# Gates and branch merges of two transformer blocks, token-major in place of feature-major

## The chip, the cores and the metric

The kernel runs on one core of one Trainium2 chip. The metric is the device time of one execution in microseconds (us), taken as the median of several runs; lower is better.

## What is computed

256 tokens with 1024 features go through two blocks, all in float32. Each block projects the normalised input, computes two branches, gates each branch with a sigmoid, merges them by up-projections, and projects the sum out. Cut to this:

```python
# block 1
xn = rms_norm(x, norm1_w)
z = xn @ w_in            # q, k, v ..., xr, gr, g_a (1024 columns), g_b (1024 columns)
attn = nsa_attention(...)                      # 512 features
rnn = rg_lru_branch(...)                       # 1024 features
merged = sigmoid(g_a) * (attn @ w_up_attn) + sigmoid(g_b) * (rnn @ w_up_rnn)
x = x + merged @ w_out
x = x + square(relu(rms_norm(x, norm2_w) @ mlp_w1)) @ mlp_w2
x = rms_norm(x, final_norm_w)
# block 2: a gated feed-forward, then
u = rms_norm(h, mix_norm); z = u @ w_in_2      # qa ka va qb kb vb, ga, gb
merged = sigmoid(ga) * (ya @ w_branch_a) + sigmoid(gb) * (yb @ w_branch_b)   # 512 features each
h = h + merged @ w_out_2
# a second gated feed-forward and a last norm
```

## The kernel before

**Precision.** Every float32 matmul is made of three fp32r products: weights and inputs are each split into a rounded part ("hi") and the rest ("lo"), and hi x hi, hi x lo and lo x hi are summed in PSUM.

**Weights.** All weights lie in one DRAM stream `ws` in the order in which the program uses them. The sync queue (SP) loads chunks of two pieces of 1024 columns into three `raw` buffers (`load_to`, L226). `split_to` (L238) splits each piece: ScalarE (ACT) writes `whi` (L248), VectorE (DVE) writes `wlo` (L249), five buffers each. `wt` (L253) asks for the split of the piece two ahead of the one that is wanted.

**Matmul forms.** `mmx` (L296) keeps a 128x128 weight tile stationary and streams 256 token columns, three matmuls for each (128 input rows, 128 output features); the result is feature-major (features on partitions). `mm3` (L290) is the opposite: 128 tokens of the input are stationary and weight columns are streamed; the result is token-major. `mm_wide` (L302) streams hi and lo of the input together (512 columns), then 256 more.

**Gates.** `fm1` (L1010, block 1) and its like `z2` (block 2) run `ga` and `gb` through `mmx`, one bank for each pair p of feature tiles (p = 0 to 3). The evacuation is a DVE multiplication by the per-token reciprocal norm `rbA`, broadcast along partitions, and an ACT tanh (`ev_tanh`, L984 and L985; `ev_g2`, L1408 and L1409). sigmoid(z) is 0.5 (1 + tanh(z/2)); the 0.5 is applied after the output projection.

**Merges.** `merge` (L1033) builds `m1` and `m2`. For each pair p, `mm` runs branch a or b through `mmx`, then DVE computes (1 + tanh) * branch in place (L1044). When both branches of p are done, `fin` adds them (L1050) and `split2` (L325) splits the sum into hi (ACT, L329) and lo (DVE, L330): that is `m`, feature-major, which `out_proj` (L1087, tags `wo`, `wo_0_*`) streams through `fm` (L336). `fm` with lead=2, hold=2 starts the first two pairs with the first 6 of 8 input tiles k before it finishes either.

**Order.** ORDER_1 and ORDER_2 (L156, L159) list the steps of each block by name: `ga1` is pair 1 of gate a, `mb2` pair 2 of branch b's merge, `at3` the next three pieces of attention. A scheduler then fixes one static order for each engine. PSUM has eight banks: `g` 3, `s` 2, `t` 2, `o` 1; matmuls of gates and merges use `g`, transposes use `t`.

Of the kernel before, what the change touches and what calls it, by code (L numbers as in the profile page):

```python
# [374 lines left out]
def build(nc, tc, d, out, es, dbg=None):  # L375
# [236 lines left out]
    def vg():  # L612
# [6 lines left out]
        hc = G.small((P, 2), "halfcol")  # L619
        nc.vector.tensor_scalar(out=hc, in0=S["colA"], scalar1=0.5, scalar2=None, op0=ALU.mult)  # L620
# [358 lines left out]
    def ev_tanh(key):  # L979
        def ev(p, b):  # L980
            if p == 0:
                S[key] = G.big(key)
            t = pair(S[key], p)
# [49 lines left out]
    def merge(tag, wa, wb, ka, kb, xa, xb, rows_a, rows_b):  # L1033

        done = []

        def mm(p, sfx, nk, x, key):
            b = G.ps("g", f"{tag}{sfx}{p}")
            for k in range(nk):
                for nn in range(2):  # L1040
                    wh, wl = G.wt((tag + sfx, k, 2 * p + nn))
                    G.mmx(b[:, nn * T:(nn + 1) * T], wh, wl, x(k), k == 0 and nn == 0, k == nk - 1)
            t = pair(S[key], p)
            nc.vector.scalar_tensor_tensor(out=t, in0=t, scalar=1.0, in1=v2(b), op0=ALU.add, op1=ALU.mult)  # L1044

        def fin(p):
            if tag not in S:
                S[tag] = Parts(G.big, tag)
            t = pair(S["tga"], p)
            nc.vector.tensor_tensor(out=t, in0=t, in1=pair(S["tgb"], p), op=ALU.add)  # L1050
            G.split2(*S[tag].pair(p), t)

        def branch(p, sfx):
            w, nk, x, rows = ((wa, ka, xa, rows_a), (wb, kb, xb, rows_b))[sfx == "b"]
            G.step(lambda: mm(p, sfx, nk, x, "tg" + sfx),
                   [((tag + sfx, k, n), w, rows(k), [(n * P, P)]) for k in range(nk) for n in (2 * p, 2 * p + 1)])
            if p in done:
                G.step(lambda: fin(p))
            done.append(p)
# [343 lines left out]
    def ev_g2(key):  # L1403
        def ev(p, b):
            if p == 0:
                S[key] = G.big(key + "2")
            t = pair(S[key], p)
            nc.vector.scalar_tensor_tensor(out=t, in0=v2(b), scalar=0.5, in1=two(S["rbA"]), op0=ALU.mult, op1=ALU.mult)  # L1408
            nc.scalar.activation(out=t, in_=t, func=AF.Tanh)  # L1409
        return ev  # L1410

# [8 lines left out]
    def take2():  # L1420
# [6 lines left out]
    g2a, g2b = ev_g2("tga"), ev_g2("tgb")  # L1427
    m2 = merge("m2", "w_branch_a_2", "w_branch_b_2", 4, 4, lambda k: S["ya"].both(k), lambda k: S["yb"].both(k), plain, paired)
# [4 lines left out]
        "ga": lambda p: z2("ga2", 2304, p, g2a), "gb": lambda p: z2("gb2", 3328, p, g2b),  # L1433
        "ma": lambda p: m2(p, "a"), "mb": lambda p: m2(p, "b"), "at": lambda n: [take2() for _ in range(n)]}
# [147 lines left out]
```

## Time and profile before

| | |
|---|---|
| device time, three runs | 966.12, 966.34, 968.51 us (median 966.34) |
| the profiled execution | 966.17 us, of which its span is 964.4 us |
| mean granted TensorE clock | 0.996 |
| TensorE (PE) busy | 948.3 us, 98% of the span |
| DVE busy | 728.4 us, 76% |
| ACT busy | 585.0 us, 61% |

The profile page gives busy time by engine, the span in 40 slices, the chain of work that ended last, and the costliest groups of instructions. A view of waits lists, by engine and line, idle time and what ended it; a timeline lists single instructions; a table of windows gives busy time and the granted TensorE clock of chosen stretches. Matmuls are pipelined, so a record's own duration overlaps its neighbours'; the price of one in a stream is the length of an unbroken piece of the chain divided by its count.

### The profile page before, as it was taken

How to read it: one execution, taken by the hardware profiler on the slowest of the kernel's cores; microseconds unless marked ns; L12 is line 12 of the kernel's file. 1: busy time of each engine (PE TensorE's matmuls, PEld its weight loads, DVE VectorE, ACT ScalarE, POOL GpSimd, SP SyncE). 2: the span in 40 equal slices, each digit the busy share in tenths (PEclk: the TensorE clock that was granted, in tenths of full speed). 3: DMA queues.
4: the chain of work that ended last, by engine and by line, in shares of the span. 5: the costliest groups of instructions: out<-in, count | busy, mean ns of one | idle time of the engine just before them, and what ended most of it. 6: DMA issues, size and time to landing. Idle time of an engine off the chain costs nothing.

```text
span 964.4 us, 15990 instructions
## 1 busy us (share of the span) xinstructions
PE 948.3 (98%) x6310; PEld 870.1 (90%) x6310; DVE 728.4 (76%) x1219; ACT 585.0 (61%) x961; POOL 42.0 (4%) x71
## 2 busy tenths in 40 slices
PE   8999999999999999999999999899999999999997
PEld 7989999998888888888888889899999888888897
DVE  7898879879888655679888657779767878777553
ACT  6795898546767544566555445678764565555441
POOL 6100000000000000030000200000000000000000
PEclk9999999999999999999999999999999999999999
DMA  9575442634545555565555755353334565555541
GB/s 331 188 268 212 138 154 104 245 131 178 215 175 193 201 177 196 195 207 180 203 187 182 240 180 177 136 204 108 113 132 172 178 201 204 185 175 183 186 141 45
DMA packets 26556, 174.03 MB, mean 180 GB/s; under 512 B 3313, under 2 KB 3569, under 8 KB 7281
## 3 DMA queue, kind: packets, MB, share of 16 engines
q1 hardware_dynamic: 24912, 169.80, 49.8%
q0 software_dynamic: 1136, 2.63, 1.4%
q8 instruction: 49, 0.80, 0.3%
q10 hardware_dynamic: 432, 0.58, 0.2%
q14 instruction: 27, 0.21, 0.1%
HBM read 171.43 MB, written 1.05 MB: 179 GB/s over the span
## 4 chain that ended last, share of the span: by engine, by line
PE 93%; ACT 4%; DVE 1%; issue 1%; DMA 0%; POOL 0%; POOLq 0%; ACTq 0%
PE f L306 17%; PE w L306 12%; PE f L307 9%; PE w L307 6%; PE ld L294 6%; PE ga L300 5%; PE fd L306 4%; PE gb L300 4%; PE wo L306 3%; PE m1b L300 2%; PE fd L307 2%; PE xr L300 2%; PE gr L300 2%; PE wo L307 2%; PE va L294 1%; PE ka L300 1%
## 5 line engine op out<-in xcount | busy, mean ns | idle before, releaser
L249 DVE TENSOR_TENSOR wlo<-raw,whi 128x1024 fp32r<-128x1024 f32 (+3 forms) x322 | 389.1, 1210 | 168.0 <-ACT whi L248 150.3
L248 ACT ACTIVATE whi<-raw 128x1024 fp32r<-128x1024 f32 (+3 forms) x322 | 335.7, 1047 | 285.6 <-PE w L306 64.2
L306 PE MATMUL f<-u,whi 128*128 128x512 f32 x704 | 246.7, 396 | 0.0
L307 PE MATMUL f<-u,wlo 128*128 128x256 f32 x704 | 196.5, 279 | 0.0
L306 PEld LDWEIGHTS f<-u,whi 128*128 128x128 f32 x704 | 132.0, 188 | 31.3
L307 PEld LDWEIGHTS f<-u,wlo 128*128 128x128 f32 x704 | 132.7, 188 | 0.1
L306 PE MATMUL w<-u,whi 128*128 128x512 f32 x256 | 88.8, 392 | 0.0
L306 PE MATMUL w<-hid,whi 128*128 128x512 f32 x256 | 88.8, 391 | 0.0
L307 PE MATMUL w<-hid,wlo 128*128 128x256 f32 x256 | 71.7, 280 | 0.0
L307 PE MATMUL w<-u,wlo 128*128 128x256 f32 x256 | 71.3, 280 | 0.0
L306 PE MATMUL fd<-f1h,whi 128*128 128x512 f32 x176 | 61.1, 394 | 0.0
L294 PE MATMUL ld<-whi,f2h 128*128 128x256 f32 (+1 forms) x264 | 59.0, 319 | 0.0
L306 PEld LDWEIGHTS w<-hid,whi 128*128 128x128 f32 x256 | 47.9, 187 | 10.5
L306 PEld LDWEIGHTS w<-u,whi 128*128 128x128 f32 x256 | 47.7, 187 | 10.3
L300 PE MATMUL ga<-u,whi 128*128 128x256 f32 x256 | 48.2, 284 | 1.1 <-ACT whi L248 1.1
L307 PE MATMUL fd<-f1h,wlo 128*128 128x256 f32 x176 | 48.8, 277 | 0.0
L307 PEld LDWEIGHTS w<-u,wlo 128*128 128x128 f32 x256 | 48.3, 189 | 0.2
L307 PEld LDWEIGHTS w<-hid,wlo 128*128 128x128 f32 x256 | 48.4, 189 | 0.0
L300 PE MATMUL gb<-u,whi 128*128 128x256 f32 x256 | 48.2, 284 | 0.0
L294 PEld LDWEIGHTS ld<-whi,f2h 128*128 128x128 f32 x264 | 44.0, 191 | 3.4
L306 PE MATMUL wo<-m,whi 128*128 128x512 f32 x128 | 44.3, 393 | 0.0
L294 PE MATMUL ld<-wlo,f2h 128*128 128x256 f32 (+1 forms) x132 | 42.1, 319 | 0.0
(533 smaller groups left out, 1924.5 us busy)
## 6 DMA issues: line engine op xcount, KB each, us to landing
raw<-in_ws_dram SPq DMA_DIRECT2D x150, 1024.0 KB, 4.8
raw<-in_ws_dram SPq DMA_DIRECT2D x3, 960.0 KB, 4.8
raw<-in_ws_dram SPq DMA_DIRECT2D x2, 992.0 KB, 4.9
nar<-in_rpb_dram POOLq DMA_DIRECT2D x16, 96.0 KB, 6.0
raw<-in_ws_dram SPq DMA_DIRECT2D x4, 256.0 KB, 6.4
raw<-in_ws_dram SPq DMA_DIRECT2D x2, 512.0 KB, 7.0
raw<-in_ws_dram SPq DMA_DIRECT2D x1, 932.0 KB, 5.1
res<-in_x_dram SPq DMA_DIRECT2D x2, 384.0 KB, 6.2
```

The source lines that it names most:

```text
L248: self.hi_ins.append(nc.scalar.activation(out=hi[:, :w], in_=src, func=AF.Copy))
L249: nc.vector.tensor_tensor(out=lo[:, :w], in0=src, in1=hi[:, :w].bitcast(F32), op=ALU.subtract)
L294: mm(out, a, b, start=start and r == 0, stop=stop and r == 2, skip_group_check=True)
L300: mm(out, a, b, start=start and r == 0, stop=stop and r == 2, skip_group_check=True)
L306: mm(bank.rearrange("p (a t) -> p a t", a=2), wh, x, start=start, stop=False, skip_group_check=True)
L307: mm(bank[:, :T], wl, x[:, 0, :], start=False, stop=stop, skip_group_check=True)
```

## The change

Gates and merges become token-major. `tok` replaces `fm1`/`z2` for `ga` and `gb` and the `mm` of `merge`: 128 tokens of the input are stationary, 512 weight columns are streamed. Output columns come in two halves c, the two halves of the tokens i have one bank each, and a step covers 4 of the input tiles k (or all 4 where there are only 4). In the last step of a half the token halves come one after the other, i=0 first. The gate's evacuation is a single ACT tanh straight from PSUM with a per-token scale that lies along partitions (`half_col`, made once in each block). The merge multiplies and adds token-major, and `turn` transposes the sum back on TensorE: 4 transposes of 128x128 for each pair p into a `t` bank, from which `split2` reads. Both ORDER tables are rewritten for the new steps, and `out_proj` starts three pairs with 4 of the 8 input tiles (lead=3, hold=4). The weights are the same bytes in another order.

```diff
-ORDER_1 = """... cw4 at1 cw5 ga0 cw6 cw7 xr2 cmp_hT cmp_fin cmp_w2
-xr3 at1 ga1 cmp_attn ga2 at3 gr0 lru0 lru1 ga3 lru2 lru3 at1 gr1 at2 gr2 gr3 exp sqrt bt at1 gelu gb0 at1 scan0 at1
-scan1 gb1 gb2 scan2 at2 scan3 gb3 at1 mb0 at1 mb1 at1 mb2 ma0 mb3 ma1 ma2 ma3"""
+ORDER_1 = """... cw4 at1 cw5 ga0 cw6 ga1 cw7 xr2 cmp_hT cmp_fin cmp_w2
+xr3 at1 ga2 cmp_attn ga3 at3 gr0 lru0 lru1 lru2 lru3 at1 gr1 at2 gr2 gr3 exp sqrt bt at1 gelu gb0 at1 scan0 at1
+gb1 scan1 gb2 scan2 at2 scan3 gb3 at1 mb0 at1 mb1 at1 mb2 mb3 ma0 ma1"""
-ORDER_2 = """... qb1 at1 ga0 at1 kb at4 ga1 at2 ga2 at4 gb0 at1 gb1 gb2 gb3 ma0 ma1 mb0 ga3 mb1
-ma2 mb2 ma3 mb3"""
+ORDER_2 = """... qb1 at1 ga0 ga1 at1 kb at4 ga2 at2 ga3 at4 gb0 gb1 at1 gb2 ma0 gb3
+ma1 mb0 mb1"""
...
+    def tok(tag, name, c0, nk, x, ev, rows=None):
+        rows = rows or (lambda k: [(k * P, P)])
+        st = {}
+        def part(n):
+            c, h = divmod(n, nk // 4)
+            ks = range(4 * h, 4 * h + 4)
+            end = ks[-1] == nk - 1
+            def fn():
+                if h == 0:
+                    st[c] = [G.ps("g", f"{tag}{c}{i}") for i in range(2)]
+                ws = {k: G.wt((tag, k, c)) for k in ks} if end else None
+                for k, i in ([(k, i) for i in range(2) for k in ks] if end else [(k, i) for k in ks for i in range(2)]):
+                    wh, wl = ws[k] if end else G.wt((tag, k, c))
+                    xh, xl = (a[:, i * P:(i + 1) * P] for a in x(k))
+                    G.mm3(st[c][i], wh, wl, xh, xl, k == 0, k == nk - 1)
+                    if k == nk - 1:
+                        ev(c, i, st[c][i])
...
-            nc.vector.tensor_tensor(out=t, in0=v2(b), in1=two(S["rbA"]), op=ALU.mult)
-            nc.scalar.activation(out=t, in_=t, func=AF.Tanh, scale=0.5)
+            nc.scalar.activation(out=S[key][:, i, c * 512:(c + 1) * 512], in_=b, func=AF.Tanh, scale=S["half" + hc][:, i:i + 1])
...
+        def ev(key):
+            def fn(c, i, b):
+                t = S[key][:, i, c * 512:(c + 1) * 512]
+                nc.vector.scalar_tensor_tensor(out=t, in0=t, scalar=1.0, in1=b, op0=ALU.add, op1=ALU.mult)
+                if (c, i) in done:
+                    fin(c, i)
+                done.append((c, i))
+            return fn
+        def fin(c, i):
+            t = S["tga"][:, i, c * 512:(c + 1) * 512]
+            nc.vector.tensor_tensor(out=t, in0=t, in1=S["tgb"][:, i, c * 512:(c + 1) * 512], op=ALU.add)
+            if i:
+                turn(c)
+        def turn(c):
...
+            for p in (2 * c, 2 * c + 1):
+                b = G.ps("t", f"{tag}T{p}")
+                for e in range(2):
+                    for i in range(2):
+                        f = (2 * p + e) * P
+                        nc.tensor.transpose(b[:, e * T + i * P:e * T + (i + 1) * P], S["tga"][:, i, f:f + P], S["ident"])
+                G.split2(*S[tag].pair(p), v2(b))
...
-        G.fm(tag, name, 8, 4, x, ev)
+        G.fm(tag, name, 8, 4, x, ev, lead=3, hold=4)
...
     def mix_fin():
         norm_fin("acc1", "A")
+        half_col("2")
```

**Block 1, from the merge to the output projection.** In these rows `m1a` is branch a's merge bank, `m1T` a bank of transposes, `m_0` and `m_1` the split sum, `wo` the output projection; numbers tell buffers apart. TensorE before, the end of the last merge bank and what follows it:

```order
L300 MATMUL m1a_2698<-q_311,whi_2632 128x256 x2
L300 MATMUL m1a_2698<-q_311,wlo_2633 128x256
L300 MATMUL m1a_2698<-q_311,whi_2632 128x256 x2
L300 MATMUL m1a_2698<-q_311,wlo_2633 128x256
L306 MATMUL wo_0_2733<-m_0_2566,whi_2665 128x512
L307 MATMUL wo_0_2733<-m_0_2566,wlo_2666 128x256
```

TensorE of the change at the same place:

```order
L294 MATMUL m1a_2355<-whi_2307,q_311 128x512 x2
L294 MATMUL m1a_2355<-wlo_2308,q_311 128x512
L294 MATMUL m1a_2355<-whi_2307,q_311 128x512
L1092 MATMUL m1T_2339<-ident,tga 128x128
L1092 MATMUL m1T_2347<-ident,tga 128x128
L1092 MATMUL m1T_2339<-ident,tga 128x128 x3
L1092 MATMUL m1T_2347<-ident,tga 128x128 x3
L1092 MATMUL m1T_2394<-ident,tga 128x128
L306 MATMUL wo_0_2409<-m_0_2344,whi_2356 128x512
L307 MATMUL wo_0_2409<-m_0_2344,wlo_2357 128x256
```

Transposes now stand between the last merge matmul and the first `wo`, and the first of pair 2 (`m1T_2394`), which takes the `t` bank of pair 0 (`m1T_2339`), stands ahead of it too. DVE before, from the first split of `m_0` on (2664 and 2698 are the last two banks of branch a):

```order
L330 TENSOR_TENSOR m_0_2566<-tga,m_0_2566 128x512
L1050 TENSOR_TENSOR tga<-tga,tgb 128x512
L1044 SCALAR_TENSOR_TENSOR tga<-tga,m1a_2664 128x512
L249 TENSOR_TENSOR wlo_2758<-raw_2630,whi_2757 128x1024
L1050 TENSOR_TENSOR tga<-tga,tgb 128x512
L330 TENSOR_TENSOR m_0_2566<-tga,m_0_2566 128x512
L1044 SCALAR_TENSOR_TENSOR tga<-tga,m1a_2698 128x512
```

DVE of the change; banks 2299 and 2300 are c=0, 2354 and 2355 are c=1:

```order
L1071 SCALAR_TENSOR_TENSOR tga<-tga,m1a_2299 128x512
L1079 TENSOR_TENSOR tga<-tga,tgb 128x512
L1071 SCALAR_TENSOR_TENSOR tga<-tga,m1a_2300 128x512
L1071 SCALAR_TENSOR_TENSOR tga<-tga,m1a_2354 128x512
L249 TENSOR_TENSOR wlo_2412<-raw_2267,whi_2411 128x1024
L1079 TENSOR_TENSOR tga<-tga,tgb 128x512 x2
L249 TENSOR_TENSOR wlo_2436<-raw_2305,whi_2435 128x1024
L1071 SCALAR_TENSOR_TENSOR tga<-tga,m1a_2355 128x512
L249 TENSOR_TENSOR wlo_2458<-raw_2305,whi_2457 128x1024
L330 TENSOR_TENSOR m_0_2344<-m1T_2339,m_0_2344 128x512
L330 TENSOR_TENSOR m_0_2344<-m1T_2347,m_0_2344 128x512
```

Before, both splits of `m_0` stand ahead of the last bank's multiplication; now all four multiplications, three additions and three `wlo` stand ahead of the first.

**Block 2, the same handover.** DVE of the change, where `m2b` is branch b, the last to be merged here (7488 and 7489 are c=0, 7543 and 7544 c=1):

```order
L1071 SCALAR_TENSOR_TENSOR tgb<-tgb,m2b_7489 128x512
L249 TENSOR_TENSOR wlo_7552<-raw_7452,whi_7551 128x1024
L1079 TENSOR_TENSOR tga<-tga,tgb 128x512
L1071 SCALAR_TENSOR_TENSOR tgb<-tgb,m2b_7543 128x512
L1079 TENSOR_TENSOR tga<-tga,tgb 128x512
L249 TENSOR_TENSOR wlo_7611<-raw_7490,whi_7610 128x1024
L1071 SCALAR_TENSOR_TENSOR tgb<-tgb,m2b_7544 128x512
L249 TENSOR_TENSOR wlo_7633<-raw_7490,whi_7632 128x1024
L330 TENSOR_TENSOR m_0_7533<-m2T_7528,m_0_7533 128x512
```

The order is of the same kind with one `wlo` and one addition fewer between the third bank and the split. On TensorE two of the eight transposes of c=0 now stand inside bank 7544's matmuls, and the other six and the first of pair 2 behind them:

```order
L294 MATMUL m2b_7544<-wlo_7497,yb_7169 128x512
L294 MATMUL m2b_7544<-whi_7496,yb_7169 128x512
L1092 MATMUL m2T_7528<-ident,tga 128x128 x3
L1092 MATMUL m2T_7536<-ident,tga 128x128 x3
L1092 MATMUL m2T_7583<-ident,tga 128x128
L306 MATMUL wo_0_0_7598<-m_0_7533,whi_7496 128x512
```

**Block 1, the first gate.** Here `cmph` is a product of the compressed attention that is mixed in, and `u` the normalised input. TensorE before, the start of gate a; one piece of weights (`whi_806`) feeds eight groups of three matmuls:

```order
L300 MATMUL ga_867<-u_0_123,whi_806 128x256 x2
L300 MATMUL ga_867<-u_0_123,wlo_807 128x256
L300 MATMUL ga_867<-u_0_123,whi_806 128x256 x2
L300 MATMUL ga_867<-u_0_123,wlo_807 128x256
L300 MATMUL ga_867<-u_0_123,whi_806 128x256 x2
L300 MATMUL ga_867<-u_0_123,wlo_807 128x256
L300 MATMUL ga_867<-u_0_123,whi_806 128x256 x2
L300 MATMUL ga_867<-u_0_123,wlo_807 128x256
L300 MATMUL ga_867<-u_0_123,whi_806 128x256 x2
```

TensorE of the change, from the first use of the piece's low part on:

```order
L294 MATMUL ga_867<-wlo_807,u_0_123 128x512
L294 MATMUL ga_867<-whi_806,u_0_123 128x512
L294 MATMUL ga_867<-whi_855,u_0_123 128x512
L673 MATMUL cmph<-whi_869,cmpB 64x256
L294 MATMUL ga_867<-wlo_856,u_0_123 128x512
L294 MATMUL ga_867<-whi_855,u_0_123 128x512 x2
L294 MATMUL ga_867<-wlo_856,u_0_123 128x512
L294 MATMUL ga_867<-whi_855,u_0_123 128x512
L294 MATMUL ga_867<-whi_887,u_1_132 128x512
L673 MATMUL cmph<-wlo_870,cmpB 64x256
L673 MATMUL cmph<-whi_869,cmpB 64x256
L673 MATMUL cmph<-wlo_870,cmpB 64x256
```

The same piece now feeds two groups of three for token half i=0, and the next piece follows at once; the other half of the tokens (`ga_868`) comes after all four pieces of c=0.

## Rows read from the trace of the kernel before

**Rows 1.** The page: busy time by engine, and the chain that ended last, by engine.

```profile
PE 948.3 (98%) x6310; PEld 870.1 (90%) x6310; DVE 728.4 (76%) x1219; ACT 585.0 (61%) x961; POOL 42.0 (4%) x71
...
PE 93%; ACT 4%; DVE 1%; issue 1%; DMA 0%; POOL 0%; POOLq 0%; ACTq 0%
```

**Rows 2.** Waits on TensorE: line, what it waited for, total us, times, longest us.

```profile
PE ka L300 <- DVE qa L1255: 3.3, 1, 3.3
PE kcvc L300 <- ACT whi L248: 1.6, 1, 1.6
...
PE ga L300 <- ACT whi L248: 1.1, 1, 1.1
```

**Rows 3.** Groups of matmuls by line and form: out<-in, shapes, count | busy us, mean ns.

```profile
L300 PE MATMUL ga<-u,whi 128*128 128x256 f32 x256 | 48.2, 284 | 1.1 <-ACT whi L248 1.1
...
L300 PE MATMUL m1b<-rnn,whi 128*128 128x256 f32 x128 | 24.9, 286 | 0.0
```

**Rows 4.** The chain in order of time at 741 to 748 us: start, length, what.

```profile
744.25 2.88 PE m2b L300 x24
747.13 0.23 PE wo L306
```

**Rows 5.** The same view at 895 to 965 us, the last matmuls.

```profile
895.01 7.50 PE ld L294 x33
902.50 0.87 PE htok L1458 x8
```

**Rows 6.** The same view at 196 to 210 us, block 1's handover.

```profile
197.68 10.08 PE m1a L300 x84
207.75 0.23 PE wo L306
```

**Rows 7.** Timeline of DVE at 204 to 216 us: start, duration, instruction.

```profile
206.12 0.68 DVE L1044 SCALAR_TENSOR_TENSOR tga<-tga,m1a 128x512 f32<-128x512 f32 x1
206.72 1.22 DVE L249 TENSOR_TENSOR wlo<-raw,whi 128x1024 fp32r<-128x1024 f32 x1
207.85 0.69 DVE L1050 TENSOR_TENSOR tga<-tga,tgb 128x512 f32<-128x512 f32 x1
208.45 0.69 DVE L330 TENSOR_TENSOR m<-tga,m 128x512 fp32r<-128x512 f32 x1
```

**Rows 8.** Timeline of DVE at 56 to 80 us.

```profile
59.95 1.18 DVE L249 TENSOR_TENSOR wlo<-raw,whi 128x1024 fp32r<-128x1024 f32 x1
...
61.57 2.35 DVE L249 TENSOR_TENSOR wlo<-raw,whi 128x1024 fp32r<-128x1024 f32 x2
...
64.51 1.22 DVE L249 TENSOR_TENSOR wlo<-raw,whi 128x1024 fp32r<-128x1024 f32 x1
...
67.36 1.22 DVE L249 TENSOR_TENSOR wlo<-raw,whi 128x1024 fp32r<-128x1024 f32 x1
...
73.62 0.17 DVE L841 TENSOR_TENSOR fn<-fn,gateA 128x6 f32<-128x6 f32 x1 [0.35 <-POOL gateA L639]
...
75.10 1.40 DVE L795 TENSOR_SCALAR attn<-attn,fn 128x128 f32<-128x128 f32 x6
...
77.01 0.61 DVE L795 TENSOR_SCALAR attn<-attn,fn 128x256 f32<-128x256 f32 x2
```

**Rows 9.** Timeline of POOL (GpSimd) at 60 to 80 us.

```profile
70.47 3.11 POOL L639 COPY gateA<-gates 128x8 f32<-128x8 f32 x3 [38.16 <-DVE gates L634]
```

**Rows 10.** Table of windows: busy by engine (count), granted TensorE clock, DMA share, GB/s.

```profile
57.00:60.00 3.00, 1.49 (x12) 1.03 (x10) 2.17 (x6) 3.00 (x8) 0.00 (x0) 1.00 0.95 306
...
614.10:615.40 1.30, 1.30 (x11) 1.30 (x12) 1.27 (x3) 1.25 (x3) 0.00 (x0) 1.00 0.72 296
615.40:618.70 3.30, 3.30 (x18) 3.30 (x18) 3.17 (x5) 3.18 (x6) 0.00 (x0) 0.50 0.45 184
```

**Rows 11.** Timeline of DVE at 604 to 617 us, the norm ahead of block 2's projections.

```profile
606.87 0.16 DVE L466 TENSOR_SCALAR v_A<-sscA 128x2 f32<-128x2 f32 x1
608.66 1.16 DVE L249 TENSOR_TENSOR wlo<-raw,whi 128x960 fp32r<-128x960 f32 x1 [1.63 <-ACT whi L248]
```

More of the change, by code (lines that the diff above doesn't have):

```diff
@@ L618, in vg @@
         gts = keep("gates", (P, 2, 24))
-        hc = G.small((P, 2), "halfcol")
-        nc.vector.tensor_scalar(out=hc, in0=S["colA"], scalar1=0.5, scalar2=None, op0=ALU.mult)
+        half_col("1")
+        hc = S["half1"]
         banks = [G.ps("g", f"vg{i}") for i in range(2)]
@@ L977, in rnn_scan, with half_col, ev_gate, ev @@
         G.split2(*S["rnn"].pair(p), S["rg"][:, sl, :])
[L979 to L983, printed above, removed]
-            nc.vector.tensor_tensor(out=t, in0=v2(b), in1=two(S["rbA"]), op=ALU.mult)
-            nc.scalar.activation(out=t, in_=t, func=AF.Tanh, scale=0.5)
+    def tok(tag, name, c0, nk, x, ev, rows=None):
[15 more added lines that the diff above has]
+                        ev(c, i, st[c][i])
+            G.step(fn, [((tag, k, c), name, rows(k), [(c0 + c * 512, 512)]) for k in ks])
+        return part
+    def half_col(name):
+        hc = G.small((P, 2), "halfcol" + name)
+        nc.vector.tensor_scalar(out=hc, in0=S["colA"], scalar1=0.5, scalar2=None, op0=ALU.mult)
+        S["half" + name] = hc
+    def ev_gate(key, hc):
+        def ev(c, i, b):
+            if key not in S or S[key, "of"] != hc:
+                S[key] = G.big(key, shape=(P, 2, D))
+                S[key, "of"] = hc
+            nc.scalar.activation(out=S[key][:, i, c * 512:(c + 1) * 512], in_=b, func=AF.Tanh, scale=S["half" + hc][:, i:i + 1])
         return ev
@@ L1035, in merge @@
         done = []
[L1037 to L1046, printed above, removed]
+        def ev(key):
[6 more added lines that the diff above has]
+            return fn
@@ L1047, in fin @@
+        def fin(c, i):
[4 more added lines that the diff above has]
+        def turn(c):
             if tag not in S:
                 S[tag] = Parts(G.big, tag)
[L1049 to L1059, printed above, removed]
@@ L1066, in build @@
+        return tok(tag + "a", wa, 0, ka, xa, ev("tga"), rows_a), tok(tag + "b", wb, 0, kb, xb, ev("tgb"), rows_b)
+    m1a, m1b = merge("m1", "w_up_attn", "w_up_rnn", 4, 8, lambda k: (S["q"][:, 0, k, :], S["q"][:, 1, k, :]),
+                     lambda k: S["rnn"].tile(k), paired, None)
     PARTS_1 = {
@@ L1401, in b2_tail @@
             G.split2(*S["y" + kind].pair(j // 2), v2(S["o2"]))
[L1403 to L1410, printed above, removed]
     attn2 = [("a", j) for j in range(4)] + [("b", j) for j in range(4)]
@@ L1425, in take2 @@
             G.step(lambda: b2_tail(br, j))
-    g2a, g2b = ev_g2("tga"), ev_g2("tgb")
-    m2 = merge("m2", "w_branch_a_2", "w_branch_b_2", 4, 4, lambda k: S["ya"].both(k), lambda k: S["yb"].both(k), plain, paired)
+    u3t = lambda k: S["u3"].tile(k)
+    g2a, g2b = (tok(key + "2", W2, c, 8, u3t, ev_gate("t" + key, "2")) for key, c in (("ga", 2304), ("gb", 3328)))
+    m2a, m2b = merge("m2", "w_branch_a_2", "w_branch_b_2", 4, 4, lambda k: S["ya"].tile(k), lambda k: S["yb"].tile(k), None, paired)
     PARTS_2 = {
@@ L1432, in build @@
         "qb": lambda p: z2("qb", 1536, p, ev_qb, lambda n: [(1536 + n * 64, 64), (1792 + n * 64, 64)]),
-        "ga": lambda p: z2("ga2", 2304, p, g2a), "gb": lambda p: z2("gb2", 3328, p, g2b),
-        "ma": lambda p: m2(p, "a"), "mb": lambda p: m2(p, "b"), "at": lambda n: [take2() for _ in range(n)]}
+        "ga": g2a, "gb": g2b, "ma": m2a, "mb": m2b, "at": lambda n: [take2() for _ in range(n)]}
     STEPS_2 = {
```

18 lines of the change are left out of this document (7 added, 11 removed).

## The prediction

> **What bounds the kernel now.** I read the page first. TensorE (PE) is busy for 98% of the span and makes 93% of the chain that ended last [rows 1], so only PE's own work and PE's waits can move the time. The list of PE's waits comes next: it names one wait of 3.3 us (block 2, behind a norm), 1.6 us at the start, 1.1 us ahead of gate `ga`, and nothing at all at `gb`, the merges or `wo` [rows 2]. The chain around the two handovers from merge to output projection shows this as rows that join without a gap: 24 merge matmuls end at 747.13 us where `wo` begins [rows 4], and 84 end at 207.76 where block 1's `wo` begins [rows 6]. So before, DVE's and ACT's part of gates and merges is wholly hidden, and any new wait of PE there is paid in full.
>
> **The change, part by part.**
>
> *Streaming.* A gate or a merge has 8 feature tiles x k input tiles x 3 products. k is 8 for the four gates and `m1b`, 4 for `m1a`, `m2a`, `m2b`: 4 x 192 + 192 + 3 x 96 = 1248 matmuls of 256 columns (the rows give x256 with `whi` for one gate name, that is two blocks, and x128 for `m1b` [rows 3]; the products with `wlo` are half as many again). They become 624 of 512 columns. An unbroken piece gives the price of each: 2.88 us / 24 = 0.120 us for 256 columns [rows 4] and 7.50 us / 33 = 0.227 us for 512 in the same operand order as `tok` [rows 5]. That is 149.8 us before, 141.6 us after: **-8.1 us**.
>
> One rule of the Trainium skill speaks against this term. "TensorE: Matmul & The Clock Gate", section "Back-to-back issue gap", gives an isolated spacing of columns/2.4 + 2.5 ns, which is an estimate of 109 and 216 ns here and a gain of 1.6 us instead. The two rows are this kernel's own streams, so the sum goes by them.
>
> *Transposes.* 8 for each half, two halves, two blocks: 32, at 0.87 us / 8 = 0.109 us [rows 5]: **+3.5 us** of PE.
>
> *Gate evacuation and merge arithmetic.* 16 DVE multiplications of 0.68 us go; 16 tanh, 16 multiplications, 8 additions and 8 splits stay, the splits now reading PSUM. PE did not wait for any of it, so I cost it at nothing; the cover is PE's streams of five to ten us between steps. If it were gone, one DVE operation costs 0.60 us (starts 206.12 and 206.72 [rows 7]). `half_col` in block 2 falls into 1.63 us in which DVE is idle [rows 11]: nothing. SP loads the same bytes.
>
> *Handover of block 1.* From the DVE starts [rows 7] a 512-wide operation occupies DVE for 0.60 us and a `wlo` for 1.13 (206.72 to 207.85); a result is there 0.68 after its start. Count from the end of bank 2354's matmuls, when bank 2300 has ended just before and DVE still has about 0.15 us of it to do. Up to the split of `m_0`, DVE's order then holds two multiplications, two additions and three `wlo`: 0.15 + 4 x 0.60 + 3 x 1.13 = 5.95 us, and the split's own 0.69 makes 6.6. PE meanwhile has 12 matmuls (2.72 us) and 8 transposes (0.87), 3.6 us. The next transpose needs the bank that this split frees, and `wo` stands behind it. PE idles for 6.6 - 3.6 = **+3.0 us**. From below: 1.9 if one `wlo` is already done when it is counted; from above: 4.1 if DVE arrives one `wlo` late. I take the walk.
>
> *Handover of block 2.* From the end of bank 7543, PE has 12 matmuls and 8 transposes (two of the first inside), of which the last matmul ends at 2.9 us. The multiplication of bank 7544 can start only behind that and behind `wlo_7611`; ready weights put it at about 3.0. Then 0.60 + 1.13 + 0.69 = 2.4 us to the end of the split: 5.4 against PE's 3.6: **+1.9 us** (0.8 without that `wlo`, 3.0 with one more).
>
> *First gate.* Before, a piece of weights feeds 24 matmuls, 2.9 us; in the change's pass over i=0 it feeds 6 of 512, 1.36 us, while DVE's `wlo` come as before: from 59.95, two from 61.57, the next at 64.51 [rows 8]. The first is done at 61.1. PE then has 5 matmuls (1.14) and a `cmph` (0.12): it wants the second `wlo` at 62.4 and gets it at 62.7. Six more and 7 `cmph` later, at 65.0, it wants the third, which ends at 65.7. The fourth is in time; PE ends the pass at 68.4, and the other half of the tokens needs no new weights: 24 matmuls, 7 `cmph` and the first two of `xr` take it to 74.9. There the first `wlo` of `xr` now stands on DVE behind the attention scaling, which waits for GpSimd's three copies of 3.11 us [rows 9]: gate factors at 68.5 (behind the `wlo` that starts at 67.36), copies to 72.1, scaling of 1.40 + 0.61 [rows 8] less overlaps, 1.13 of `wlo`: 75.3. That is 0.3 + 0.7 + 0.4, less about 0.2 that this stretch waits already: **+1.2 us** (0.4 to 2.0).
>
> *Other gates and merges.* The same burst of weight demand recurs in `gr`/`gb` of block 1 and in block 2's attention. The trace has no such pass elsewhere; its nearest rows are waits for weights of 1.1 and 1.6 us [rows 2], and nothing below zero, since there is no wait to remove. Elsewhere a full step of work lies between, and DVE has slack: **+0.6 us** for both, 0 to 3.2.
>
> *The clock.* After the 3.3 us wait of rows 2 PE ran at full speed for 1.3 us and then at the lower of its two levels (0.50, 1.2 of 2.4 GHz) for 3.3 us, with 18 matmuls where the pace ahead of it (11 in 1.30) gives 28: 1.2 us lost, or 1.65 as half of the stretch [rows 10]. After the 1.1 us wait the clock stayed at 1.00 [rows 10]. The new 3.0 us is nearest to the first, so I count one drop at block 1's handover, **+1.4 us** (0 to 1.65), and none at block 2's.
>
> Sum: -8.1 + 3.5 + 3.0 + 1.9 + 1.2 + 0.6 + 1.4 = +3.5 us. The profiled execution took 966.17 us, so 969.7; the median of the runs lies 0.17 above it: **969.9 us**.
>
> **The rivals.** 0.3% (2.9 us) is about what a measurement can tell from no change.
>
> 1. *The handovers are covered* (not slower). The first 24 pairs of `wo` need only c=0's sum, which was finished a step earlier; if DVE gets to its split ahead of the `wlo` rows, PE never waits. Then -4.6 + 1.2 + 0.6 gives -2.8 and, with the first gate covered too, -4.6: 961.7 to 963.5. Against it: DVE works in the order shown, and `wlo` and multiplications of the last bank stand ahead of the split. It decides if DVE is over 3 us ahead there.
> 2. *No drop of the clock.* Everything as forecast, but 3.0 us idle is short enough: +2.1, 968.4. For it: 1.1 us was. Against: 3.3 us was not.
> 3. *Weights arrive late in the other gates too.* ACT and DVE each split a piece in about 1.1 us and share the time with attention; two waits of the size of rows 2 add 2.5 us: 972.4.
> 4. *A second drop of the clock,* after block 2's 1.9 us: 971.3.
> 5. *A column costs the same in both forms* here: 512 columns at twice 0.120, no gain from streaming, 978.0. The price of 0.227 in rows 5 speaks plainly against it. The rule of the Trainium skill named above comes near it and would give 976.4.
> 6. *Nothing moves*: a scheduler that hides the waits by exactly what is gained, 966.
>
> **How the numbers follow.** The forecast has 0.36, of which 0.28 lies over +0.3% (969.2). Rival 1 has 0.15 (0.13 of it faster than 963.4), rival 2 0.21 (0.17 same, 0.04 slower), rival 3 0.14, rival 4 0.07, rival 5 0.03 (all slower), rival 6 0.04 (same). Faster 0.13; same 0.08 + 0.02 + 0.17 + 0.04 = 0.31; slower 0.28 + 0.04 + 0.14 + 0.07 + 0.03 = 0.56. The range starts below rival 6 and the forecast's low ends (the sum with handovers of 1.9 and 0.8, 0.4 at the gate, nothing for the rest, no drop, is 964.8; all at once is unlikely, so 965.5) and ends above rival 3, at 973.5: it leaves out rivals 1 and 5 and little else.
>
> **What would show it.** In the profile of the changed kernel: 512-column pieces of gates and merges at 0.227 us each; PE waits listed at `wo` (or the `m1T` row ahead of it) for DVE L330, about 3 us, and near 2 us at `m2T`/`wo_0_0`; waits of `ga` and `xr` for `wlo` adding to 1 us more than before; 3.3 us at 0.50 soon after block 1's handover; the 3.3 us of `ka` unchanged. Wrong I would be if PE shows no wait at the handovers, if the clock stays at 1.00 after them, or if waits for weights above 1 us appear at `gb` or in block 2.

## The result and the profile after

The changed kernel takes **984.03 us** (median of four runs, 982.22 to 985.47) against 966.93 (966.12 to 968.51) for the kernel before in the same runs: ratio 1.0176, 95% interval 1.0163 to 1.019. The prediction had the side right (slower, 969.9) and the size wrong: 17 us more, not 3.5, and outside its range of 965.5 to 973.5.

The profiled execution has a span of 982.8 us, 18.4 more than before. The page's first part answers to [rows 1]:

```profile
PE 956.8 (97%) x5718; PEld 846.2 (86%) x5718; DVE 722.7 (74%) x1204; ACT 589.1 (60%) x961; POOL 39.2 (4%) x71
```

TensorE makes 592 matmuls fewer and is nevertheless busy for longer. The list of waits on TensorE answers to [rows 2] (line, what it waited for, total us, times, longest us):

```profile
PE gb L294 <- ACT tgb L1017: 3.1, 2, 2.1
PE m1T L1092 <- DVE m L330: 3.1, 1, 3.1
...
PE m2T L1092 <- DVE m L330: 2.0, 1, 2.0
...
PE o_b L1431 <- DVE ptb10l L330: 1.2, 1, 1.2
...
PE ga L294 <- DVE wlo L249: 0.3, 1, 0.3
```

None of these five stood in the list of before; together they are 9.7 us. The two handovers are there with 3.1 and 2.0 us. The largest surprise of the list is `gb`, which waits for ACT's tanh. Next the table of windows, after, which answers to [rows 10] (its columns are the same; the granted clock is the third from the end):

```profile
209.50:215.50 6.00, 5.54 (x18) 4.78 (x19) 1.60 (x3) 0.00 (x0) 0.00 (x0) 0.50 0.48 175
300.00:400.00 100.00, 100.00 (x568) 86.67 (x567) 64.52 (x81) 52.80 (x72) 0.00 (x0) 1.00 0.53 184
440.00:530.00 90.00, 90.00 (x512) 78.08 (x511) 74.95 (x105) 52.99 (x84) 0.26 (x1) 1.00 0.54 188
626.00:632.00 6.00, 5.64 (x26) 5.67 (x27) 5.53 (x9) 5.56 (x9) 0.00 (x0) 0.50 0.48 172
727.90:731.30 3.40, 3.34 (x8) 2.66 (x9) 1.98 (x4) 2.81 (x6) 0.00 (x0) 0.51 0.00 0
```

and two windows of the same length in the trace of before, in stages that the change doesn't touch:

```profile
300.00:400.00 100.00, 100.00 (x579) 88.18 (x578) 62.46 (x76) 52.30 (x70) 0.00 (x0) 1.00 0.54 189
440.00:530.00 90.00, 90.00 (x521) 78.79 (x520) 74.88 (x104) 53.12 (x85) 0.00 (x0) 1.00 0.53 189
```

Two things are to be seen. The clock is at 1.2 GHz (0.50) in three stretches in which TensorE works, one at the first handover, one at the old 3.3 us wait at `ka`, one at the wait at `gb`; before there was one, of which [rows 10] shows 3.3 us. By the granted clock the three last 6.8, 6.8 and 3.4 us, the one of before 3.4. And in 100 us of unedited feed-forward, with TensorE busy throughout and the clock at 1.00, it gets through 568 matmuls instead of 579. The starts show why. There a pair of matmuls (512 columns, then 256) has either a mean spacing of **346.7 ns** or one of **353.3 ns** (the mean time from one pair's start to the next), in a pattern that repeats every three pairs and holds for 50 to 180 us without a break. Before, block 1's two feed-forward products and block 2's first feed-forward run at 346.7 and block 2's last at 353.3; in this execution after, it is the reverse in all of them.

The difference of the two profiled executions, term by term:

| term | us | from |
|---|---|---|
| gate and merge streams | -6.9 | starts of all their matmuls, waits taken off: 151.9 before, 145.0 after |
| 32 transposes | +3.4 | starts, waits taken off |
| PE's waits | +10.0 | the five above, and 2.5 instead of 2.2 for weights at the program's start |
| half-speed stretches | +6.0 | half of the time that PE worked in them: 7.7 (of 209.1 to 216.0, 625.6 to 632.4, 728.0 to 731.4) against 1.7 |
| spacing in unedited stages | +4.5 | first start of a stage to first start of the next: 181.4 against 178.3, 187.7 against 184.6, 123.0 against 124.7 |
| not assigned | +1.4 | rest of 18.4 |

The handover of block 1 went by the walk. DVE's timeline, after, answers to [rows 7]:

```profile
202.81 1.28 DVE L1071 SCALAR_TENSOR_TENSOR tga<-tga,m1a 128x512 f32<-128x512 f32 x2
204.01 1.22 DVE L249 TENSOR_TENSOR wlo<-raw,whi 128x1024 fp32r<-128x1024 f32 x1
205.14 1.29 DVE L1079 TENSOR_TENSOR tga<-tga,tgb 128x512 f32<-128x512 f32 x2
206.35 1.22 DVE L249 TENSOR_TENSOR wlo<-raw,whi 128x1024 fp32r<-128x1024 f32 x1
207.49 0.68 DVE L1071 SCALAR_TENSOR_TENSOR tga<-tga,m1a 128x512 f32<-128x512 f32 x1
208.08 1.22 DVE L249 TENSOR_TENSOR wlo<-raw,whi 128x1024 fp32r<-128x1024 f32 x1
209.22 1.28 DVE L330 TENSOR_TENSOR m<-m1T,m 128x512 fp32r<-128x512 f32 x2
```

and TensorE's at the same place:

```profile
205.82 1.04 PE L1092 MATMUL m1T<-ident,tga 128*128 128x128 f32 x8
209.96 0.47 PE L1092 MATMUL m1T<-ident,tga 128*128 128x128 f32 x1 [3.11 <-DVE m L330]
```

The eight transposes start at 205.82; the next one starts 3.11 us after they have ended, when the first of the two splits that begin at 209.22 is done. Ahead of it stand the multiplications, additions and three `wlo`, in the order that is shown ahead of the prediction.

The wait at `gb` is of another kind. ACT's timeline, after, in block 2:

```profile
724.20 0.51 ACT L268 ACTIVATE attb<-attb,nmb 128x256 f32<-128x256 f32 x1 [2.12 <-DVE nmb L1405]
...
726.28 0.57 ACT L329 ACTIVATE ptb20h<-ptb 128x512 fp32r<-128x512 f32 x1
726.76 0.58 ACT L329 ACTIVATE yb<-o_b 128x512 fp32r<-128x512 f32 x1
727.24 1.25 ACT L1017 ACTIVATE tgb<-gb,halfcol 128x512 f32<-128x512 f32 x2
728.38 0.91 ACT L793 ACTIVATE attb<-attb,fb 128x256 f32<-128x256 f32 x2
```

and TensorE's row that waits for it:

```profile
727.96 0.80 PE L294 MATMUL gb<-whi,u 128*128 128x512 f32 x1 [2.08 <-ACT tgb L1017]
```

The last of the 48 matmuls of gate b's first half starts at 715.08. Its two tanh come to the front of ACT's queue only at 727.24, behind softmax rows that themselves wait for DVE and behind two splits; ACT even stands idle for 2.12 us in between, while both banks are full. Until the first tanh has read its bank, the second half has no second `g` bank (15 of its matmuls have gone into the third one by then, in the program's order), and PE stands with the rest of the gate behind it: its next `gb` starts 0.05 us after the first tanh has ended. Block 1 shows the same at 160 us, for 1.0 us. The wait at `o_b` comes earlier, at 723.55, and is for a split on DVE; no run isolates what made it.

### The profile page after: what moved, and what is told of

Its sections match the earlier page's. It is cut to its first block, busy times and chain, and to the rows that moved or that the text cites. A ratio compares the mean times of both kernels' runs of the same rounds, so it can differ in the third digit from the quotient of the medians.

```text
span 982.8 us, 14781 instructions
## 1 busy us (share of the span) xinstructions
PE 956.8 (97%) x5718; PEld 846.2 (86%) x5718; DVE 722.7 (74%) x1204; ACT 589.1 (60%) x961; POOL 39.2 (4%) x71
## 5 line engine op out<-in xcount | busy, mean ns | idle before, releaser
L249 DVE TENSOR_TENSOR wlo<-raw,whi 128x1024 fp32r<-128x1024 f32 (+4 forms) x322 | 388.8, 1210 | 175.8 <-ACT whi L248 156.0
L248 ACT ACTIVATE whi<-raw 128x1024 fp32r<-128x1024 f32 (+4 forms) x322 | 335.8, 1048 | 277.6 <-PE w L306 69.1
L306 PE MATMUL wo<-m,whi 128*128 128x512 f32 x128 | 47.9, 415 | 0.0
L294 PE MATMUL gb<-whi,u 128*128 128x512 f32 x128 | 43.3, 404 | 3.1 <-ACT tgb L1017 3.1
L294 PE MATMUL ga<-whi,u 128*128 128x512 f32 x128 | 41.7, 395 | 1.1 <-ACT whi L248 1.1
```

The lines of the kernel that those rows point to most:

```text
L248: self.hi_ins.append(nc.scalar.activation(out=hi[:, :w], in_=src, func=AF.Copy))
L249: nc.vector.tensor_tensor(out=lo[:, :w], in0=src, in1=hi[:, :w].bitcast(F32), op=ALU.subtract)
L294: mm(out, a, b, start=start and r == 0, stop=stop and r == 2, skip_group_check=True)
L306: mm(bank.rearrange("p (a t) -> p a t", a=2), wh, x, start=start, stop=False, skip_group_check=True)
```

## The experiments

Theory after the result: the new waits cost what the list says, and the rest of the loss lies outside the change, in the clock and in which of two spacings the unedited stages get. The first two runs repeat the kernels unedited.

**rep_after.** No edit.

> The changed kernel again, unedited. Theory: the pair of a feed-forward stream (512 columns, then 256) has two spacings, 346.7 and 353.3 ns, and which one a stage gets is set by the order of instructions ahead of it, so this profile shows again 353.3 in block 1's two feed-forward products and block 2's first one, 346.7 in block 2's last, and about 984 us. Rival: each execution draws its spacing by chance; then some stage shows the other value here, and the profiled executions differ by 2 to 4 us.

Measured: 977.17 us (973.29 to 983.39, four executions; ratio 1.0133, 1.0096 to 1.017). The profiled one took 973.29. Its waits are the same to 0.1 us at `gb`, `m1T`, `m2T` and `o_b`; its windows are not:

```profile
211.10:214.60 3.50, 3.50 (x14) 2.96 (x13) 0.00 (x0) 0.00 (x0) 0.00 (x0) 0.54 0.62 255
300.00:400.00 100.00, 100.00 (x579) 88.15 (x578) 64.10 (x80) 53.99 (x74) 0.00 (x0) 1.00 0.55 190
440.00:530.00 90.00, 90.00 (x521) 78.83 (x520) 75.44 (x104) 53.40 (x85) 0.00 (x0) 1.00 0.55 189
619.20:626.00 6.80, 6.80 (x56) 6.71 (x57) 5.15 (x8) 6.55 (x11) 0.00 (x0) 1.00 0.34 141
```

579 and 521 matmuls where the first profile had 568 and 512, one half-speed stretch (211.4 to 214.8) instead of three, none behind `ka` (the wait ends at 619.2 here, and 619.2 to 626 is at 1.00). The theory that the program fixes the spacing falls: one and the same kernel has executions 10 to 12 us apart, with the same waits in the two that were profiled. Chance is not the whole of it either, as the next run shows.

**rep_before.** No edit.

> The kernel before again, unedited. Theory: 346.7 ns for the pair everywhere but in block 2's last feed-forward (353.3), one half-speed stretch of 3.6 us, 966 to 967 us. Rival (chance): another spacing in some stage, and with it 2 to 4 us more or less; the half-speed stretch behind the 3.3 us wait twice as long is possible too (+1.4 us).

Measured: 966.28 us (965.76 to 968.55, ten executions; ratio 1.0006, 0.9996 to 1.0015). The spacing is that of the first profile in every stage, and the executions of before beside the other kernels lie between 964.5 and 968.8 (one of 1891.7 apart, which no profile shows), so none has the 10 us by which those of the change differ. The half-speed stretch at `ka` is twice as long as in the first profile (612.6 to 619.4), with the same wait of 3.3 us, in which it begins:

```profile
612.60:616.00 3.40, 2.05 (x9) 2.08 (x10) 3.34 (x7) 2.09 (x4) 0.00 (x0) 0.50 0.67 224
616.00:619.40 3.40, 3.40 (x17) 3.40 (x17) 3.18 (x5) 3.28 (x6) 0.00 (x0) 0.50 0.23 89
```

So the length of such a stretch varies between executions of one program.

**half0_first.** Branch a's first half is merged ahead of the second halves.

```diff
-gb1 scan1 gb2 scan2 at2 scan3 gb3 at1 mb0 at1 mb1 at1 mb2 mb3 ma0 ma1"""
+gb1 scan1 gb2 scan2 at2 scan3 gb3 at1 mb0 at1 mb1 at1 ma0 mb2 mb3 ma1"""
...
-... gb0 gb1 at1 gb2 ma0 gb3
-ma1 mb0 mb1"""
+... gb0 gb1 at1 gb2 gb3
+ma0 mb0 ma1 mb1"""
```

> Only the order tables differ from the changed kernel: in both blocks branch a's first half is merged before the second halves (block 1: mb0 mb1 ma0 mb2 mb3 ma1; block 2: gb2 gb3 ma0 mb0 ma1 mb1). Theory: DVE then has the first sum split before the last bank in block 2 (wait of 2.0 us gone), in block 1 the split still stands behind two wlo and the last multiplication (wait 3.1 to about 1.8); with the half-speed stretch behind it shorter or gone: 976 to 982 us. Rival (the handover wait comes from the transposes themselves and not from the order): both waits as before, 984 us.

Measured: 970.68 us (970.29 to 971.91; ratio 1.0047, 1.0032 to 1.0062), below the range that was expected. The waits moved less than expected, `m1T` 3.1 to 2.7 and `m2T` 2.0 to 1.1; `gb` 2.8; `o_b` gone. The half-speed stretch at block 1's handover stays (209.5 to 213). All three feed-forward stages have 346.7 ns. Against the 973.29 of rep_after, with the same spacing there, the profiled execution (970.91) gains 2.4 us although it has one such stretch more; the waits alone are 2.8 us less. Against the median of the change most of the 13 us is not the order's.

**split_first.** Three `wlo` of the output projection behind the first split.

```diff
+        self.first, self.n_first = None, 0
...
-            nc.vector.tensor_tensor(out=lo[:, :w], in0=src, in1=hi[:, :w].bitcast(F32), op=ALU.subtract)
+            wlo = nc.vector.tensor_tensor(out=lo[:, :w], in0=src, in1=hi[:, :w].bitcast(F32), op=ALU.subtract)
+            if self.first is not None:
+                if p >= self.n_first + 2:
+                    self.behind(wlo, self.first)
+                if p >= self.n_first + 4:
+                    self.first = None
...
-                G.split2(*S[tag].pair(p), v2(b))
+                lo = G.split2(*S[tag].pair(p), v2(b))
+                if p == 0:
+                    G.first, G.n_first = lo, G.n_split
```

> The changed kernel with one rule more for DVE's order: at each handover the third to fifth wlo of the output projection stand behind the first split of the merged sum instead of ahead of it. Theory: the waits of 3.1 and 2.0 us fall to about 1.4 each (what is left is multiply, add, and the split's ACT and DVE halves behind the last bank), and the clock stays up at block 1's handover (3.0 us less): 978 to 981 us. Rival (wlo are not the cause, the last multiplication or the transposes are): 3.1 and 2.0 as before, 984 us. Clock rival: the wait falls and the half-speed stretch stays, 981 to 982.

Measured: 977.87 us (977.28 to 979.29; ratio 1.0121, 1.0106 to 1.0136). The waits fell to 1.5 (`m1T`) and 1.4 (`m2T`), as expected, and the clock stayed up at the handover:

```profile
209.50:215.50 6.00, 6.00 (x37) 5.33 (x36) 4.17 (x6) 1.27 (x3) 0.00 (x0) 1.00 0.81 294
300.00:400.00 100.00, 100.00 (x569) 86.76 (x568) 62.61 (x78) 52.23 (x71) 0.00 (x0) 1.00 0.53 185
...
815.00:885.00 70.00, 70.00 (x397) 60.66 (x397) 54.29 (x75) 41.61 (x63) 0.00 (x0) 1.00 0.53 187
```

So the `wlo` ahead of the split are what made 2.2 us of the two waits, and with 1.5 us idle in place of 3.1 there was no stretch at 0.50. That the shorter wait kept the clock up is not shown by this pair alone: imajor, below, has 3.1 us there and no stretch. Over all profiles the waits of 2.7 us and more at this place brought a stretch four times in five, those of 1.5 to 1.7 us in none of five. The time came out a little below the range that was expected, and so near by luck. Two things that the expectation did not count nearly cancel in this profile: block 2's last feed-forward is at 353.3 ns like the others (2.3 us more), and the clock's stretch at `gb` is gone and that at `ka` halved (3.1 us less). The other three executions took 1 to 2 us less; their spacing is not known.

**imajor.** All parts of a gate or merge run one token half after the other.

```diff
-                ws = {k: G.wt((tag, k, c)) for k in ks} if end else None
-                for k, i in ([(k, i) for i in range(2) for k in ks] if end else [(k, i) for k in ks for i in range(2)]):
-                    wh, wl = ws[k] if end else G.wt((tag, k, c))
+                ws = {k: G.wt((tag, k, c)) for k in ks}
+                for k, i in [(k, i) for i in range(2) for k in ks]:
+                    wh, wl = ws[k]
```

> The changed kernel, but every part of a gate or merge runs token half i=0 through its four input tiles before i=1 (the change does so only in a half's last part). Theory for the 3.1 us of waits at gate b: the second bank of c=1 is wanted one group after c=0 ends, while ACT stands with the tanh that frees it behind another instruction; 12 matmuls (2.7 us) on the third bank first cover that, so the waits for ACT tgb fall from 3.1 us to under 0.5, and 2 to 4 us go. Rival (weights): the pass over i=0 now wants a piece each 1.36 us in all parts, and waits for whi or wlo take their place: no gain or slower. In both cases the stream spacing of the unedited stages may be 346.7 or 353.3 and is read separately.

Measured: 976.01 us (969.87 to 979.25; ratio 1.0101, 1.0071 to 1.0131), too spread to read the edit from the time. The waits can be read:

```profile
PE gb L294 <- ACT tgb L1017: 1.1, 1, 1.1
PE ga L294 <- ACT whi L248: 1.1, 1, 1.1
```

`gb` fell from 3.1 to 1.1, `o_b` is gone, and no wait for weights has come in (that of `ga` stands in [rows 2] too). The reason expected for it was wrong, however. In the program's order the changed kernel itself already runs 24 matmuls of the third bank (block 1) and 15 (block 2) before it wants the bank that ACT frees; in imajor they are 19 and 15. What moved is the rest of the order. In block 1 the two tanh run 1.6 us earlier, and attention matmuls stand ahead of the second bank's first `gb`, so that PE comes to it (158.45) just as the first tanh has ended; in block 2 they still come late:

```profile
157.73 1.25 ACT L1017 ACTIVATE tgb<-gb,halfcol 128x512 f32<-128x512 f32 x2
...
714.13 1.24 ACT L1017 ACTIVATE tgb<-gb,halfcol 128x512 f32<-128x512 f32 x2
...
714.85 0.50 PE L294 MATMUL gb<-whi,u 128*128 128x512 f32 x1 [1.12 <-ACT tgb L1017]
```

Wherever PE waits at `gb`, in both kernels, it starts again 0.05 us after the first tanh has ended. So the bank that ACT frees late is what PE waits for; no run moves the tanh alone. The clock contradicts the readings so far: behind the same 3.1 us wait at block 1's handover it stays at 1.00 here, and a stretch at 0.50 comes behind the 1.1 us wait at `ga`, which brought none in any other profile.

```profile
61.10:64.40 3.30, 3.28 (x8) 2.62 (x9) 3.30 (x6) 3.30 (x7) 0.00 (x0) 0.50 0.68 231
209.50:215.50 6.00, 6.00 (x37) 5.29 (x38) 2.09 (x4) 1.28 (x3) 0.00 (x0) 1.00 0.50 175
```

**combo_hold.** half0_first with the rule for three `wlo`, counted from the output projection's first pieces.

> The order of half0_first with split_first's rule for three wlo of the output projection. Theory: m1T waits 1.4 us instead of 2.7, m2T under 1 instead of 1.1, and with 1.4 us idle no half-speed stretch at block 1's handover: 1.7 us less; at the spacing of 346.7 ns as in half0_first 967 to 969 us, at 353.3 in all stages up to 9 more. Rival (the clock falls by more than the handover's wait): the half-speed stretch stays at about 210 us.

Measured: 975.43 us (973.6 to 975.74; ratio 1.008, 1.0058 to 1.0102). `m1T` waits 1.7 (1.4 was expected), `m2T` not at all, but `wo` 0.8 for a split, and the clock is at 1.00 from 209 to 216 us. Block 1's feed-forward and block 2's first one are at 353.3 ns, which is 6.9 us of the 9 that the expectation allowed for this.

**split_tick.** split_first, with one transpose more at each norm, six in all.

```diff
             nc.tensor.transpose(b[:, i * P:(i + 1) * P], col[:, i:i + 1].to_broadcast([P, P]), S["ident"])
+        nc.tensor.transpose(b[:, T:T + P], col[:, 1:2].to_broadcast([P, P]), S["ident"])
```

> split_first with one more 128-column transpose, which nothing reads, behind the two of each norm's broadcast: about 0.6 us more work on TensorE in all. Theory: which spacing a feed-forward stage gets is set at the last short matmuls put into its stream, so one more of them can send the stages from 353.3 to 346.7 ns, and the whole falls by 3 to 9 us against split_first's 977.9 though work was added. Rival (the token-major streams ahead, memory or heat slow the stages): they stay at 353.3 ns and it takes 978.5.

Measured: 971.78 us (969.7 to 973.87, ten executions; ratio 1.0055, 1.0041 to 1.0069): 6 us less than split_first, with work added and the same waits to 0.1 us. The windows of split_first above are now

```profile
300.00:400.00 100.00, 100.00 (x579) 88.15 (x578) 62.78 (x77) 52.60 (x71) 0.00 (x0) 1.00 0.55 190
...
815.00:885.00 70.00, 70.00 (x406) 61.72 (x406) 55.87 (x78) 41.78 (x62) 0.00 (x0) 1.00 0.54 190
```

All three feed-forward stages went from 353.3 to 346.7 ns. Between the two profiled executions (979.29 and 969.7) the pairs make 8.2 us of the 9.6, and the clock another 1.6: here no stretch follows the wait at `ka`. In the traces nearly every lasting change of spacing stands at the short matmuls of a norm (2 columns, then 128) that are put into the stream (in combo and combo_hold one stands at the transposes `htok`); behind them one of the two patterns sets in and stays. That the spacing costs whole stages, and that it can be moved without touching gates or merges, is shown; why a given place yields one or the other is not.

**before_lead.** The kernel before with the change's lead and hold alone.

```diff
-        G.fm(tag, name, 8, 4, x, ev)
+        G.fm(tag, name, 8, 4, x, ev, lead=3, hold=4)
```

> The kernel before with one part of the change alone: lead=3, hold=4 in the output projections. Theory: there was no wait at the handover to cover, so 966 to 967 us if the stream spacing stays (346.7 but for block 2's last feed-forward); another spacing in some stage moves it by 2 to 9 us. Rival (lead and hold themselves cost, by more banks held and later residuals): waits at wo or behind it that before does not have, over 1 us.

Measured: 965.12 us (963.6 to 966.33, ten executions; ratio 0.9977, 0.9966 to 0.9987). No new wait. The last feed-forward is at 346.7 ns instead of 353.3 (352 pairs x 6.7 ns = 2.3 us), `wo` in both blocks at 353.3 instead of 346.7 (0.9 us). So lead and hold cost nothing themselves, and this is the fastest kernel of the study, by the spacing.

**combo.** half0_first, the rule for three `wlo` and i-major parts together.

> All three edits on the changed kernel: half0_first's order, the rule for three wlo, and i-major parts. Theory: of PE's new waits (gb 3.1, m1T 3.1, m2T 2.0, o_b 1.2) about 1.1, 1.7 and 0.8 are left, no half-speed stretch at block 1's handover; with 346.7 ns in the three feed-forward stages 965 to 967 us, with 353.3 in all of them 9 more. Rival (waits move elsewhere: weights of an i-major pass, or another bank): waits for whi or wlo of over 1 us that imajor and combo_hold do not show.

Measured: 973.16 us (972.02 to 974.49; ratio 1.0069, 1.0054 to 1.0084). The waits left are `m1T` 1.7, `wo` 0.8 and `gb` 0.4, with none for weights beyond those of the change. The first three feed-forward products (block 1's two, block 2's first) are at 353.3 ns, the last is mostly at 346.7.

**combo_tick.** combo with the extra transpose.

> combo with split_tick's one more transpose behind each norm's broadcast. Theory: the waits as in combo, 0.6 us more work; the spacing of the feed-forward stages is drawn anew, so this differs from combo by whole stages of 2 to 3.4 us and not by 0.6. Rival (spacing follows from the waits or the clock ahead): the same spacings as combo and 0.6 us more.

Measured: 967.27 us (966.9 to 968.23, ten executions; ratio 1.0008, 0.9998 to 1.0019), 5.9 us below combo. The waits are combo's, the stages all at 346.7 ns. With its stalls repaired the token-major form comes level with the kernel before, no further: against before_lead, which has the same spacing in these stages, it is 2.1 us slower (six extra transposes of 0.11 us are in that).

**after_tick and before_tick.** The extra transpose in the changed kernel and in the one before.

> The changed kernel with one more unread transpose behind each norm's broadcast (about 0.6 us of work). Theory: the short matmuls redraw the spacing of the feed-forward stages; if they all get 346.7 ns this shows the change without that part of its cost: waits as before (gb 3.1, m1T 3.1, m2T 2.0, o_b 1.2), one to three half-speed stretches, 973 to 977 us. If some keep 353.3: 2 to 3.4 us more for each. Rival (the whole 17 us is in the waits and the clock): 983 to 985 us with 346.7 ns everywhere.

> The kernel before with the same extra transposes. Theory: before's own stages are redrawn too; at 346.7 ns in all it gains 2.0 us in block 2's last feed-forward and pays 0.6: 964.5 to 966 us; at 353.3 in one of block 1's stages 968 to 970. With after_tick it gives the price of the change at equal spacing, expected 8 to 10 us. Rival (the extra transpose always helps, whatever the kernel): before gains as much as split_first did, 6 us.

Measured: 978.34 us (975.35 to 981.09, six executions; ratio 1.0111, 1.009 to 1.0132) and 970.01 (969.52 to 972.31; ratio 1.0032, 1.0019 to 1.0046). The extra transpose is no cure: it made before 3.3 us slower, which answers the rival. By luck the two profiled executions have the same spacing in all three stages, 353.3 in block 1's, 346.7 in block 2's first, 353.3 in its last. Windows of after_tick:

```profile
300.00:400.00 100.00, 100.00 (x567) 86.75 (x567) 63.52 (x80) 53.55 (x73) 0.00 (x0) 1.00 0.54 189
440.00:530.00 90.00, 90.00 (x521) 78.78 (x520) 75.93 (x104) 53.68 (x86) 0.00 (x0) 1.00 0.56 193
815.00:885.00 70.00, 70.00 (x398) 60.70 (x397) 55.19 (x75) 40.91 (x63) 0.00 (x0) 1.00 0.54 191
```

and of before_tick:

```profile
300.00:400.00 100.00, 100.00 (x567) 86.66 (x566) 62.45 (x77) 51.09 (x68) 0.00 (x0) 1.00 0.52 185
440.00:530.00 90.00, 90.00 (x521) 78.71 (x520) 75.29 (x103) 53.06 (x86) 0.00 (x0) 1.00 0.56 196
815.00:885.00 70.00, 70.00 (x399) 60.70 (x398) 54.87 (x75) 39.56 (x62) 0.00 (x0) 1.00 0.54 187
```

The medians differ by 8.3 us, but the spacing is read in one execution of each only. Those two (980.88 and 969.89) differ by 11.0, of which 3.3 are the clock: after_tick has three half-speed stretches (one of them behind the wait at `m2T`, at 759 us), before_tick one. A cleaner pair are the profiled executions of rep_after (973.29) and before_lead (965.01), both at 346.7 ns in these stages, at 353 in the output projections, and with one half-speed stretch each: **8.3 us**. By the starts that is -6.5 for the gate and merge streams, +3.4 for the transposes, +9.8 for PE's waits, and 1.6 for the rest.

## Why the prediction was right or wrong

- **Streaming, -8.1: -6.9.** The price held where nothing stands between (block 1's `m1a`: 48 matmuls in 10.9 us, 0.227 each). Where other matmuls are mixed in, the 512-column form lost 3.4 us to small gaps, the 256-column form 2.1. The isolated spacing that the Trainium skill states ("TensorE: Matmul & The Clock Gate", section "Back-to-back issue gap"), by which the gain would be an estimated 1.6 us, is contradicted by these rows as by those of before: it is an estimate of 0.216 and 0.109 us, where 0.227 and 0.120 are measured.
- **Transposes, +3.5: +3.4.**
- **Handovers, +3.0 and +1.9: 3.1 and 2.0.** Walk and order were right, and split_first shows the cause: moving the `wlo` behind the split took 1.6 and 0.6 us away.
- **First gate, +1.2: 0.3 of wait.** `xr` ends 6.5 us later than before; less 0.3 from the program's start and 5.1 for the 48 matmuls that stand ahead in place of 48 shorter ones, 1.1 are left, which looks like the forecast. But only one of the three waits that I walked came (0.3 at `ga`); the other 0.8 are small gaps of the 48 matmuls and of `cmph`, most of which the -6.9 above already holds. The size was luck.
- **Other gates and merges, +0.6: 4.3.** Here the prediction failed. I bounded this term by waits for weights. The resource that ran out was a PSUM bank, freed by ACT's tanh, and ACT holds its rows in order: the tanh stood behind rows that waited for DVE (3.1 us at `gb`). The other 1.2 us, at `o_b`, is a wait for DVE in the same stretch of the new order; its cause stays open. I costed the gate's evacuation at nothing because nobody had waited for it before; but before, a gate took one bank of three for each pair, and now a half takes two.
- **The clock, +1.4: +6.0 in the profile, from -1.7 (split_tick) to +3.3 (after_tick) in others.** This term failed too. The stretch at the first handover came as forecast, but a second came behind the wait at `gb`, and both the first and the old one at `ka` lasted twice as long as the row that I had priced it by. In rep_after one such stretch is all there is, and in imajor the same 3.1 us wait brought none. rep_before shows that the length at `ka` varies for before as well: the row gave one draw of it, and I took it for the price. I also read the 1.1 us wait as harmless from a row that ends 0.2 us behind it; the trace of before bears that out, imajor does not.
- **What was not in the sum: unedited stages, +4.5 in the profile.** The sum took for granted, without a reason, that code which the change does not touch takes the same time. The feed-forward stages have 1,392 pairs, each 6.7 ns longer at one spacing than at the other: 512 in block 1 (3.4 us), 528 in block 2's first (3.5), 352 in its last (2.3). Over the profiles of this study the sum over all pairs above 346.7 ns, output projections included, lies between 0.7 and 9.5 us.
- **The rivals.** Rival 1 is out (both handovers wait), rival 2 too (the clock did fall), rival 3 had the place right (the other gates) and the resource wrong. Rival 4 is what the profile shows in part, at `gb` instead of `m2T`; after_tick has it at `m2T`. Rival 5 is out by the 0.227 us of `m1a`, rival 6 by the result.

At equal spacing and with one half-speed stretch on either side the change costs 8.3 us, where the forecast said 3.5 (2.1 without its clock term). Of the measured 17 us the other 9 are, by the profiled execution, the draw of spacing and clock; the other three of the first measurement have no profile. What stays open: what decides which spacing sets in behind a norm, why before and split_first draw the same each time, by their times, and the changed kernel does not, and what makes a half-speed stretch come or not, short or long.

## What to carry to other kernels

When a change takes more PSUM banks for the same work, look at who frees them: walk the evacuating engine's static order up to the instruction that reads the bank, as one would for a handover, and don't bound that term by waits of another resource. Before crediting or blaming a change with a per cent, compare the pace of stages that it doesn't touch (matmuls in 100 us of a steady stream is enough): if that moved, repeat the kernel, or perturb it, until the paces agree.

## What the runs showed that was not expected

A steady stream of 512- and 256-column matmuls ran for 50 to 180 us at a mean of 346.7 or of 353.3 ns a pair, with the granted clock at 1.00 and no wait in either. The single starts differ too: 230 and 117 ns over and over in one pattern, 232, 236 and 240 with 118, 114 and 120 in the other. The pattern changed mostly where 2-column and 128-column matmuls of a norm were put between, and one unread transpose of 0.1 us at each norm moved whole kernels by -6.1 us (split_first), -5.9 (combo), +3.3 (before), draws of the clock included. Half-speed stretches at the same wait of 3.2 to 3.3 us lasted 3.4 us (before), 6.8 (rep_before, and the changed kernel) or did not come (rep_after, split_tick). The same wait of 3.1 us at the handover brought 6.8 us (the changed kernel), 3.4 (rep_after) or none (imajor), where a wait of 1.1 us brought one.
